# Where ff2's first blocks lie in memory, and the order in which they are loaded

## The chip, the cores and the metric

The kernel runs on one core of one Trainium2 chip. The metric is the device time of one execution in microseconds; the time before is the median of three runs. One further execution was recorded by the profiler; all rows quoted below are of that one.

The engines are TensorE (PE; its weight loads are PEld), VectorE (DVE), ScalarE (ACT), GpSimd (POOL) and SyncE (SP), whose queue issues nearly all DMAs. SBUF, the memory next to the engines, is where every tile lives; matrix products land in eight PSUM banks.

## The reference

One decoder layer on 1024 tokens of width 1024. A combined input projection feeds a recurrent group (RWKV-7, 8 heads of 64) and a causal convolution group; their outputs go through an output projection and a residual; then comes the MLP, where the change lies, and a final norm:

```python
x = x + jnp.concatenate([y_rwkv, y_conv], axis=-1) @ w_out[l]
h = rmsnorm(x, norm_mlp_g[l])
x = x + jnp.square(jax.nn.relu(h @ w_ff1[l])) @ w_ff2[l]
...
return rmsnorm(x, norm_final_g)
```

h is 1024 x 1024, w_ff1 1024 x 4096 and w_ff2 4096 x 1024, all float32. I call the two products ff1 and ff2.

## The kernel before, in words

**Precision.** A float32 product is made of three products of halves: `halves` (L848 to L853) rounds a block to a high half on ScalarE (L851) and subtracts it from the block on VectorE for the low half (L852). TensorE then multiplies high by high, high by low and low by high (L96 is the one line that issues matmuls). So every block that TensorE reads has cost one ScalarE and one VectorE instruction first: ah and al of an A block, bh and bl of a B block.

**Seven products in place of eight.** ff1 and ff2 both cut their matrices in 2 x 2 blocks and use a scheme of seven products of sums and differences (Strassen's, in Winograd's form). ff1's operand from the hidden side is kept ready split in SBUF: pool `fpa` holds the blocks B11 and B21 (mB11h, mB11l, mB21h, mB21l in the trace), pool `fpb` the sums T1 to T4 and B22. ff1 goes in 16 pairs of column blocks (`class Pair`); within a pair the products come in the order M1 (reads B11), M2 (reads B21), then M3 and M4 of the pair before, then M6, M7, M5. So in the last pair B11 and B21 are read first, and T1, B22, T4 last. Each finished block of 128 x 512 is squared ReLU on ScalarE (L871, L872) in one of three buffers `c` of pool `hd`, and written by SP to memory (L873), to one of four arrays hid_d0 to hid_d3 by the place in the 4096 hidden columns. The weights of ff1 come through four raw buffers of pool `w1p`.

**ff2.** It has four rounds r = 0 to 3, each over a quarter of the hidden columns. In round r, A is hid_d[r] and B a quarter of w_ff2; each of A11, A12, A21, A22, B11, B12, B21, B22 is loaded by `load` (L1178 to L1185 before) as two tiles c = 0, 1 of 128 x 1024 (512 KB each), with two buffers for each name. A11 and B11 have two names each, e and o, for even and odd rounds. The seven products of a round, with 48 matmuls of 128 x 512 each, are, in the program's order:

- A11·B11 and A12·B21, both added onto the output block (1,1);
- `m6`: S2·T2, where S1 = A21 + A22 and S2 = S1 - A11 are made on VectorE, T1 = B12 - B11 and T2 = B22 - T1 on GpSimd (L1189 before); added onto block (2,1);
- S1·T1, in the same banks as the product before it, then onto (2,2);
- `m7`: (A11 - A21)·(B22 - B12), then `m4`: A22·(B21 - T2), then `m3`: (A12 - S2)·B22.

`onto_x2` (L1220 before) adds a finished bank to the residual on VectorE: four instructions for each product. A product that goes on in the same bank waits for that. `ahead` issues the loads of the next round inside the round.

**Order of the work.** The program is recorded as written and then ordered by a scheduler, engine by engine, from its own cost model and from when each tile's memory is free; what stands on a queue goes out in that order. An instruction behind a waiting one on its engine waits too. SP has eight DMA semaphores in turn: a DMA waits for the one eight places before it on the queue.

**Memory.** The pools are two stacks, one from each end of SBUF. At the end of ff1 the right stack holds, from its bottom: x2 (the residual), `fpa`, `w1p`, `hd`, `fpb`. They are closed and ff2's pools are put in the same place: before, `wr` (nine names, 72 KB a partition), then `wf` (the halves ah, al, bh, bl and the sums sA, sB), then `wr3` (gf, the final norm's weights, and B11o). A new tile waits, tile by tile, until what lay in its memory has been read for the last time. Within a pool the name that was used first lies farthest from the stack's bottom: A11e, the first block that ff2 needs, lies where `hd`'s `c` buffers were, which ff1 uses to its end; A11o, needed a round later, lies on `fpa`.

Of the kernel before, what the change touches and what calls it, by code (L numbers as in the profile page):

```python
# [9 lines left out]
F32 = mybir.dt.float32  # L10
# [8 lines left out]
P = 128  # L19
# [33 lines left out]
def hymba_layer(ctx: ExitStack, tc: tile.TileContext, a: dict, out: bass.AP):  # L53
# [81 lines left out]
    right = dict(side="right", reuse_waits="tile")  # L135
# [566 lines left out]
    def open_pool(name, **kw):  # L702
        pools[name] = tc.tile_pool(name=name, bufs=1, reuse_waits="tile", **kw)
        return pools[name].__enter__()

    def close_pool(name):
        pools.pop(name).__exit__(None, None, None)
# [463 lines left out]
        close_pool(name)  # L1171


    wr = open_pool("wr", side="right")
    NR = 4
    raws = {}

    def load(r, what, i, k):  # L1178

        src = hid_d[r] if what == "A" else w_ff2_d  # L1180
        tag = f"{what}{i}{k}" + ("eo"[r % 2] if (i, k) == (1, 1) else "")
        f0, col = (4 * (k - 1), i) if what == "A" else (8 * r + 4 * (i - 1), k)
        for c in range(2):
            t = raws[r, what, i, k, c] = (wr3 if tag == "B11o" else wr).tile([P, 2, 512], F32, name=tag, bufs=2)
            nc.sync.dma_start(out=t, in_=src[:, f0 + 2 * c:f0 + 2 * c + 2, (col - 1) * 512:col * 512])  # L1185

    def sum2(engine, name, x, y, op):
# [69 lines left out]
    def quad(n):  # L1257
        return [bank(x) for x in (("ps", "ps", "ps", "pr"), ("ca", "cb", "ya", "yb"))[n % 2]]

    for args in (("A", 1, 1), ("B", 1, 1), ("A", 1, 2), ("B", 2, 1)):  # L1260
        load(0, *args)
    for args in (("A", 2, 1), ("A", 2, 2), ("B", 1, 2), ("B", 2, 2)):
        load(0, *args)
    wf = open_pool("wf", side="right")
    wr3 = open_pool("wr3", side="right")
    gf = wr3.tile([P, D], F32, name="gf")
    nc.sync.dma_start(out=gf, in_=a["norm_final_g"].partition_broadcast(P))
    for r in range(NR):
# [8 lines left out]
        def ahead(*args):  # L1277
            if not final:
                load(r + 1, *args)
# [53 lines left out]
        ahead("B", 2, 2)  # L1333
    close_pool("wr3")
    close_pool("wf")
    close_pool("wr")


_INS = ["x", "norm_mix_g", "w_in", "shift_mu", "w0", "w_decay_up", "a0", "w_aaa_up", "w_gate_up",
# [20 lines left out]
```

## Time and profile before

| | us |
|---|---|
| time before, median of three runs (1310.55 to 1310.72) | 1310.57 |
| the profiled execution's own time | 1310.69 |
| its span, first to last instruction | 1309.0 |
| TensorE busy (8107 matmuls) | 1223.2 |
| VectorE busy | 943.7 |
| ScalarE busy | 559.1 |
| GpSimd busy | 100.6 |
| ff1's last matmul starts at | 958.03 |
| ff2's first matmul starts at | 974.90 |
| ff2's last matmul starts at | 1297.76 |

All moments are counted from the span's start. A row of the timeline has the start, the duration, the engine, the line of the kernel, the operation, output <- inputs by tile name (buffer numbers left out, so ps stands for three banks), and in brackets the idle time of the engine before it with what ended that. A matmul's duration runs to the modelled end of its pipeline; its true price in a row of matmuls is the distance from start to start. "SPq" rows are DMA issues, not the transfers. In the trace all A blocks of ff2 but A11 are called A, all B blocks but B11 are called B.

### The profile page before, as it was taken

The numbers are of one execution on the slowest core, as the hardware profiler recorded it, in microseconds if no ns is written. First come the engines' busy times: TensorE is split into PE (matmuls) and PEld (weight loads), VectorE is DVE, ScalarE is ACT, GpSimd is POOL, SyncE is SP. The second block draws the span as 40 slices with busy tenths as digits, with TensorE's granted clock in tenths as the row PEclk, the third lists the DMA queues.
The fourth block names the chain that finished last, engine by engine and source line by source line (L and its number), as shares of the span: only waits on it lengthen the run. The fifth ranks groups of instructions, "written<-read, shape, count | busy, mean of one in ns | idle before, by whom it ended". The sixth has DMA issues, their size and how long they took to land.

```text
span 1309.0 us, 20808 instructions
## 1 busy us (share of the span) xinstructions
PE 1223.2 (93%) x8107; PEld 1058.3 (81%) x8107; DVE 943.7 (72%) x1639; ACT 559.1 (43%) x1001; POOL 100.6 (8%) x57
## 2 busy tenths in 40 slices
PE   5999999998998779999998999999948899999996
PEld 4999898987887668999887888888837688888885
DVE  6478796789459855655778666664429798887997
ACT  6432433433441165323577445455533233333344
POOL 1000000000000000000000000000005224232320
PEclk9999999997997587999999999999979899999998
DMA  5214426455564556533345354442266425232003
GB/s 188 57 49 108 122 66 175 106 137 128 134 168 118 124 166 182 172 105 102 93 145 185 129 163 151 152 129 98 81 226 216 145 65 161 65 96 81 17 1 129
DMA packets 194475, 161.44 MB, mean 123 GB/s; under 512 B 54386, under 2 KB 153784, under 8 KB 194376
## 3 DMA queue, kind: packets, MB, share of 16 engines
q1 hardware_dynamic: 181192, 157.90, 40.6%
q10 hardware_dynamic: 13056, 2.13, 0.9%
q8 instruction: 64, 1.05, 0.3%
q14 instruction: 35, 0.29, 0.1%
q0 software_dynamic: 128, 0.08, 0.0%
HBM read 110.23 MB, written 49.84 MB: 122 GB/s over the span
## 4 chain that ended last, share of the span: by engine, by line
PE 65%; DVE 7%; DMA 3%; ACT 2%; issue 1%; SPq 0%; ACTq 0%; DVEq 0%
PE ps L96 29%; PE yb L96 10%; PE ya L96 8%; PE cb L96 8%; PE ca L96 6%; PE pr L96 4%; DVE al L852 1%; PE ps L99 1%; DVE acc L331 1%; DVE sA L1189 1%; DMA woraw<-in_w_out_dram 1%; DVE x L1220 1%; DMA hid_d<-c 1%; DVE bl L852 1%; DVE odd L331 0%
## 5 line engine op out<-in xcount | busy, mean ns | idle before, releaser
L851 ACT ACTIVATE ah<-sA 128x1024 fp32r<-128x1024 f32 x32 | 34.0, 1061 | 135.7 <-PE pr L96 50.4
L96 PE MATMUL ps<-bh,ah 128*128 128x512 f32 x168 | 66.3, 408 | 22.4 <-ACT bh L851 16.5
L96 PE MATMUL cb<-hh,wh 128*128 128x256 f32 x248 | 72.7, 293 | 1.5 <-ACT hh L243 1.5
L96 PE MATMUL cb<-hl,wh 128*128 128x256 f32 x248 | 72.9, 294 | 0.3 <-DVE hl L244 0.3
L852 DVE TENSOR_TENSOR al<-sA,ah 128x1024 fp32r<-128x1024 f32 x32 | 55.0, 1718 | 23.5 <-ACT ah L851 23.5
L96 PE MATMUL cb<-hh,wl 128*128 128x256 f32 x248 | 71.7, 289 | 0.0
L96 PE MATMUL ps<-bl,ah 128*128 128x512 f32 x168 | 68.1, 405 | 3.7 <-DVE bl L852 3.7
L96 PE MATMUL ps<-bh,al 128*128 128x512 f32 x168 | 67.8, 403 | 0.0
L96 PE MATMUL yb<-hh,wh 128*128 128x256 f32 x232 | 67.7, 292 | 0.0
L96 PE MATMUL yb<-hh,wl 128*128 128x256 f32 x232 | 66.6, 287 | 0.0
L96 PE MATMUL yb<-hl,wh 128*128 128x256 f32 x232 | 66.5, 287 | 0.0
L851 ACT ACTIVATE w1h<-s 128x512 fp32r<-128x512 f32 x64 | 40.4, 633 | 52.6 <-PE ps L96 34.0
L852 DVE TENSOR_TENSOR w1l<-s,w1h 128x512 fp32r<-128x512 f32 x64 | 44.0, 688 | 24.8 <-ACT w1h L851 24.7
L96 PEld LDWEIGHTS ps<-bh,ah 128*128 128x128 f32 x168 | 33.0, 197 | 30.1 <-ACT bh L851 16.9
L1189 POOL TENSOR_TENSOR sB<-B,B11e 128x1024 f32<-128x1024 f32 x4 | 12.1, 3014 | 564.3 <-DMA B<-in_w_ff_dram 562.0
L871 ACT ACTIVATE c<-c 128x512 f32<-128x512 f32 x60 | 37.9, 632 | 35.6 <-DVE c L957 20.1
L96 PEld LDWEIGHTS cb<-hh,wh 128*128 128x128 f32 x248 | 48.3, 195 | 5.4 <-ACT hh L243 1.9
L96 PEld LDWEIGHTS cb<-hl,wh 128*128 128x128 f32 x248 | 48.3, 195 | 4.8 <-issue 4.0
L96 PEld LDWEIGHTS cb<-hh,wl 128*128 128x128 f32 x248 | 48.1, 194 | 2.3 <-issue 2.1
L851 ACT ACTIVATE w1h<-w1r 128x512 fp32r<-128x512 f32 x48 | 30.2, 631 | 42.5 <-PE ps L96 26.6
L852 DVE TENSOR_TENSOR w1l<-w1r,w1h 128x512 fp32r<-128x512 f32 x48 | 33.0, 689 | 19.7 <-ACT w1h L851 19.7
L96 PEld LDWEIGHTS yb<-hh,wh 128*128 128x128 f32 x232 | 44.6, 192 | 3.1 <-issue 2.1
(472 smaller groups left out, 4035.9 us busy)
## 6 DMA issues: line engine op xcount, KB each, us to landing
w1r<-in_w_ff_dram SPq DMA_DIRECT2D x44, 512.0 KB
hid_d<-c SPq DMA_DIRECT2D x64, 256.0 KB
LK<-lk_d SPq DMA_DIRECT2D x32, 384.0 KB
A<-hid_d SPq DMA_DIRECT2D x24, 512.0 KB
B<-in_w_ff_dram SPq DMA_DIRECT2D x24, 512.0 KB
wraw<-in_w_in_dram SPq DMA_DIRECT2D x22, 512.0 KB
xt<-in_x_dram SPq DMA_DIRECT2D x8, 512.0 KB
lk_d<-AR SPq DMA_DIRECT2D x16, 256.0 KB
```

The costliest lines, as they stand in the source:

```text
L96: return self._order(PE.matmul(o, lhsT=lhsT, rhs=rhs, start=start, stop=stop, skip_group_check=more))
L99: self._order(PE.transpose(o, in_, identity))
L331: return V.scalar_tensor_tensor(o, x, c, o, op0=ALU.mult, op1=ALU.add)
L851: S.activation(hi, src, AF.Copy)
L852: V.tensor_tensor(lo, src, hi.bitcast(F32), op=ALU.subtract)
L871: S.activation(c, c if src is None else src, AF.Relu)
L1189: engine.tensor_tensor(t, x, y, op=op)
L1220: V.tensor_tensor(o, o, banks[t].t, op=ALU.add)
```

## The change

Each of the nine names of `wr` gets a pool of its own, opened in the order of the list RAW, so that the first of the list lies at the bottom of the stack; and the first round's loads are issued with B12 and B22 ahead of A21 and A22 (before: behind them). Sizes and counts of tiles are the same.

```diff
-    wr = open_pool("wr", side="right")
+    RAW = ("B21", "A12", "B11e", "A11e", "A21", "B22", "B12", "A22", "A11o")
+    wr = {tag: open_pool("wr" + tag, side="right") for tag in RAW}
...
-            t = raws[r, what, i, k, c] = (wr3 if tag == "B11o" else wr).tile([P, 2, 512], F32, name=tag, bufs=2)
+            t = raws[r, what, i, k, c] = wr[tag].tile([P, 2, 512], F32, name=tag, bufs=2)
...
-    for args in (("A", 1, 1), ("B", 1, 1), ("A", 1, 2), ("B", 2, 1)):
-        load(0, *args)
-    for args in (("A", 2, 1), ("A", 2, 2), ("B", 1, 2), ("B", 2, 2)):
+    for args in (("A", 1, 1), ("B", 1, 1), ("A", 1, 2), ("B", 2, 1), ("B", 1, 2), ("B", 2, 2), ("A", 2, 1), ("A", 2, 2)):
         load(0, *args)
...
-    wr3 = open_pool("wr3", side="right")
+    wr3 = wr["B11o"] = open_pool("wr3", side="right")
...
-    close_pool("wr")
+    for tag in reversed(RAW):
+        close_pool("wr" + tag)
```

By the sizes (8 KB a partition for each name, a block of `fpa` 8 KB), B21, A12, B11e and A11e now lie on the four blocks of `fpa`, A21, B22 and B12 on `w1p`, A22 on the border of `w1p` and `hd`, and A11o on `hd`.

What the scheduler makes of it at the seam, first on SP's queue, where ff1's last writes (hid_d<-c) meet ff2's first loads. In these rows A_10043, A_10045 (now A_10067, A_10069) are A12 and B_10047, B_10049 (now B_10071, B_10073) are B21, one row for each half. Before:

```order
L873 DMA hid_d_139<-c 128x512 x10
L1267 DMA gf<-in_norm_final_g_dram 128x1024
L1185 DMA B11o<-in_w_ff_dram 128x2x512 x2
L873 DMA hid_d_139<-c 128x512
L1185 DMA A11e<-hid_d_136 128x2x512 x2
L1185 DMA B11e<-in_w_ff_dram 128x2x512 x2
L1185 DMA A_10043<-hid_d_136 128x2x512
L1185 DMA A_10045<-hid_d_136 128x2x512
L1185 DMA B_10047<-in_w_ff_dram 128x2x512
L1185 DMA B_10049<-in_w_ff_dram 128x2x512
```

And now:

```order
L873 DMA hid_d_139<-c 128x512 x5
L1186 DMA A11e<-hid_d_136 128x2x512 x2
L1186 DMA B11e<-in_w_ff_dram 128x2x512 x2
L1186 DMA A_10067<-hid_d_136 128x2x512
L873 DMA hid_d_139<-c 128x512
L1186 DMA A_10069<-hid_d_136 128x2x512
L1186 DMA B_10071<-in_w_ff_dram 128x2x512
L1186 DMA B_10073<-in_w_ff_dram 128x2x512
L873 DMA hid_d_139<-c 128x512 x4
```

The four blocks of the first two products stand ahead of the last six writes of ff1 (one of those comes further down); the rows of gf and B11o are behind them.

On ScalarE, at the same place, the splits of A11 and B11 (ah, bh) beside ff1's last activations (c). Before:

```order
L871 ACTIVATE c<-ps 128x512
L872 ACTIVATE c<-c 128x512
L871 ACTIVATE c<-c 128x512
L872 ACTIVATE c<-c 128x512
L851 ACTIVATE ah<-A11e 128x1024 x2
L851 ACTIVATE bh<-B11e 128x1024 x2
```

And now:

```order
L871 ACTIVATE c<-ps 128x512
L872 ACTIVATE c<-c 128x512
L851 ACTIVATE ah<-A11e 128x1024
L851 ACTIVATE bh<-B11e 128x1024
L851 ACTIVATE ah<-A11e 128x1024
L851 ACTIVATE bh<-B11e 128x1024
L851 ACTIVATE ah<-A_10067 128x1024
L851 ACTIVATE bh<-B_10071 128x1024
L871 ACTIVATE c<-c 128x512
L872 ACTIVATE c<-c 128x512
```

Six splits moved ahead of ff1's last block, and the halves of A11 and B11 now take turns.

The second place is the sums of round 0. On SP's queue A_10053 is the second half of A21, A_10055 and A_10057 are A22, B_10059 and B_10061 B12, B_10063 and B_10065 B22. Before:

```order
L1185 DMA A_10053<-hid_d_136 128x2x512
L1185 DMA A_10055<-hid_d_136 128x2x512
L1185 DMA A_10057<-hid_d_136 128x2x512
L1185 DMA B_10059<-in_w_ff_dram 128x2x512
L1185 DMA B_10061<-in_w_ff_dram 128x2x512
L1185 DMA B_10063<-in_w_ff_dram 128x2x512
L1185 DMA B_10065<-in_w_ff_dram 128x2x512
L1185 DMA A11o<-hid_d_137 128x2x512 x2
L1185 DMA B11e<-in_w_ff_dram 128x2x512
```

And now, where A_10085 is the second half of A21 and A_10087, A_10089 are A22 (B12 and B22 went out before these rows):

```order
L1186 DMA A_10085<-hid_d_136 128x2x512
L1266 DMA gf<-in_norm_final_g_dram 128x1024
L1186 DMA B11o<-in_w_ff_dram 128x2x512 x2
L1186 DMA B11e<-in_w_ff_dram 128x2x512
L873 DMA hid_d_139<-c 128x512
L1186 DMA B11e<-in_w_ff_dram 128x2x512
L1186 DMA A_10087<-hid_d_136 128x2x512
L1186 DMA A_10089<-hid_d_136 128x2x512
L1186 DMA A11o<-hid_d_137 128x2x512 x2
```

Ahead of A22 stand now gf, B11o, the B11 of round 2 (B11e; it goes into the buffer that round 0's B11 still holds, and waits for the last reader of each half, VectorE and GpSimd) and ff1's last write.

On VectorE, from the last splits of the second product to S2 of the first half (x_0 to x_3 are the residual's updates, sA<-A,A is S1, sA<-sA,A11e is S2, bl<-sB the low half of T2). Before:

```order
L852 TENSOR_TENSOR al<-A_10045,ah 128x1024
L1220 TENSOR_TENSOR x_0_4867<-x_0_4867,ps 128x512
L852 TENSOR_TENSOR bl<-B_10049,bh 128x1024
L1189 TENSOR_TENSOR sA<-A_10051,A_10055 128x1024
L1220 TENSOR_TENSOR x_1_4868<-x_1_4868,ps 128x512
L1220 TENSOR_TENSOR x_2_4869<-x_2_4869,ps 128x512
L1189 TENSOR_TENSOR sA<-sA,A11e 128x1024
```

And now:

```order
L852 TENSOR_TENSOR al<-A_10069,ah 128x1024
L852 TENSOR_TENSOR bl<-B_10073,bh 128x1024
L1221 TENSOR_TENSOR x_0_4867<-x_0_4867,ps 128x512
L1221 TENSOR_TENSOR x_1_4868<-x_1_4868,ps 128x512
L1221 TENSOR_TENSOR x_2_4869<-x_2_4869,ps 128x512
L1221 TENSOR_TENSOR x_3_4870<-x_3_4870,pr 128x512
L852 TENSOR_TENSOR bl<-sB,bh 128x1024
L1190 TENSOR_TENSOR sA<-A_10083,A_10087 128x1024
L1190 TENSOR_TENSOR sA<-sA,A11e 128x1024
```

The four updates and the low half of T2 now stand ahead of S1 and S2; before, two of the updates and that low half came behind.

## Prediction

> **What bounds the kernel now.** I read the page first (busy shares), then the stretches of 10 us, then the TensorE timeline at every gap, and from each gap the engine that ended it. The page's first two lines say that TensorE carries the program; the stretches around the seam between ff1 and ff2 say where it does not (columns: PE, PEld, DVE, ACT, POOL busy us, granted clock, DMA share, GB/s).
>
> ```profile
> span 1309.0 us, 20808 instructions
> ...
> PE 1223.2 (93%) x8107; PEld 1058.3 (81%) x8107; DVE 943.7 (72%) x1639; ACT 559.1 (43%) x1001; POOL 100.6 (8%) x57
> ...
> 950.00:960.00 10.00, 7.74 (x33) 5.74 (x31) 1.83 (x3) 3.87 (x7) 0.00 (x0) 1.00 0.14 52
> 960.00:970.00 10.00, 0.00 (x0) 0.00 (x0) 0.00 (x0) 1.15 (x2) 0.00 (x0) 0.66 0.74 245
> 970.00:980.00 10.00, 5.10 (x12) 4.04 (x13) 6.13 (x5) 5.41 (x6) 0.00 (x0) 0.50 1.03 374
> ...
> 1000.00:1010.00 10.00, 6.53 (x22) 4.93 (x21) 10.00 (x9) 3.90 (x4) 2.78 (x2) 0.83 0.47 157
> 1010.00:1020.00 10.00, 5.99 (x26) 4.30 (x24) 10.00 (x6) 3.85 (x4) 6.58 (x2) 1.00 0.51 152
> 1020.00:1030.00 10.00, 7.86 (x23) 6.27 (x24) 8.99 (x10) 0.27 (x1) 3.89 (x2) 0.66 0.71 235
> 1030.00:1040.00 10.00, 10.00 (x46) 8.29 (x45) 5.52 (x7) 4.02 (x4) 0.88 (x1) 1.00 0.09 34
> ```
>
> There are two holes. From 958 to 975 nothing computes and DMA works: ff2's first blocks are loading. From 1000 to 1030 VectorE is full (10.00 of 10) and TensorE is not: the sums of ff2's round 0. After 1030 TensorE has no gap of note (46 matmuls in 10 us). The TensorE timeline has the gaps; the row in brackets names who ended it.
>
> ```profile
> 958.03 0.39 PE L96 MATMUL ya<-mT4h,w1l 128*128 128x512 f32 x1
> 974.90 1.65 PE L96 MATMUL ps<-bh,ah 128*128 128x512 f32 x3 [16.48 <-ACT bh L851]
> ...
> 976.77 0.63 PE L96 MATMUL ps<-bl,ah 128*128 128x512 f32 x1
> 977.20 0.63 PE L96 MATMUL ps<-bh,al 128*128 128x512 f32 x1
> ...
> 982.96 0.39 PE L96 MATMUL ps<-bh,ah 128*128 128x512 f32 x1
> 983.18 0.39 PE L96 MATMUL ps<-bl,ah 128*128 128x512 f32 x1
> ...
> 999.28 0.84 PE L96 MATMUL ps<-bh,ah 128*128 128x512 f32 x3
> ...
> 1003.81 0.54 PE L96 MATMUL ps<-bl,ah 128*128 128x512 f32 x1 [3.47 <-DVE bl L852]
> ...
> 1022.14 0.76 PE L96 MATMUL ps<-bh,ah 128*128 128x512 f32 x1 [5.90 <-DVE x L1220]
> ```
>
> One matmul takes 0.227 us from start to start at full clock (982.96 to 983.18, rounded) and 0.43 at half (976.77 to 977.20). I call the products by their order: P1 = A11·B11 and P2 = A12·B21 (974.90 to 999.28), P3 = S2·T2 from 999.28, P4 = S1·T1 from 1022.14; each has 48 matmuls, 10.9 us at full clock.
>
> Why the first gap is 16.5 us stands on SP's queue and in the chain of waits.
>
> ```profile
> 959.17 0.33 SPq L1267 DMA_DIRECT2D gf<-in_norm_final_g_dram  x1
> ...
> 960.59 7.46 DMA hid_d<-c
> ...
> 968.52 5.25 DMA B11e<-in_w_ff_dram
> ...
> 973.79 1.07 ACT bh L851
> ```
>
> gf, then two blocks of the next round, then ff1's last output go out before A11; the second half of A11 waits for that output to be written (960.59 + 7.46), B11 goes out behind it at 968.52 and lands 5.25 us later. All of it begins after ff1's last matmul.
>
> **The change, part by part.**
>
> *Loads move into ff1.* A11, B11, A12, B21 now lie where ff1's B11 and B21 blocks were, whose last reader is the TensorE row here, beside a row of SP's queue, one of VectorE and the DMA's:
>
> ```profile
> 938.02 0.39 PE L96 MATMUL cb<-mB21h,w1l 128*128 128x512 f32 x1
> ...
> 937.40 5.66 SPq L873 DMA_DIRECT2D hid_d<-c  x3
> ...
> 952.66 0.69 DVE L957 TENSOR_TENSOR c<-u,ya 128x512 f32<-128x512 f32 x1 [2.21 <-ACT u L927]
> ...
> DMA  0000000000100000580000291008500005800000
> ```
>
> SP reaches them behind the write at 937.40, so eight 512 KB loads go out between about 938 and 942, into an almost idle DMA (the last row is its busy share from 930 to 950, in tenths). In the stretch 970 to 980 DMA moved 374 GB/s, 1.4 us a load: landed by about 951. Six microseconds are in hand before ScalarE wants them (957, below). What it could cost: the ff1 writes queued among them land later, by at most eight times 1.4 = 11 us. The next output is written at 952.66, into a buffer whose write was queued near 941: 11 us of cover. I cost it at nothing; without the cover ff1 would lose the few us by which the write is late, and no gain is possible, since ff1 ends on TensorE.
>
> *The start of ff2.* ScalarE now has six splits ahead of ff1's last activation, behind the one before it.
>
> ```profile
> 955.74 0.60 ACT L871 ACTIVATE c<-ps 128x512 f32<-128x512 f32 x1 [1.06 <-PE ps L96]
> 956.37 0.63 ACT L872 ACTIVATE c<-c 128x512 f32<-128x512 f32 x1
> ...
> 982.93 1.06 ACT L851 ACTIVATE ah<-A 128x1024 fp32r<-128x1024 f32 x1 [2.67 <-PE pr L96]
> 983.90 1.04 ACT L851 ACTIVATE bh<-B 128x1024 fp32r<-128x1024 f32 x1
> ```
>
> 957.00 + 0.97 + 1.04 = 959.01: P1 starts at 959.05 instead of 974.90, **-15.85 us**. The output that now waits behind the six splits is needed in round 3 alone.
>
> *P1 and P2* are paced by VectorE's low halves. These rows give its prices and POOL's:
>
> ```profile
> 958.46 0.69 DVE L973 TENSOR_TENSOR c<-u,ya 128x512 f32<-128x512 f32 x1 [5.11 <-PE ya L96]
> ...
> 995.32 2.82 DVE L852 TENSOR_TENSOR al<-sA,ah 128x1024 fp32r<-128x1024 f32 x1
> 998.07 3.42 DVE L1189 TENSOR_TENSOR sA<-sA,A11e 128x1024 f32<-128x1024 f32 x1
> ...
> 1010.15 1.21 DVE L852 TENSOR_TENSOR bl<-sB,bh 128x1024 fp32r<-128x1024 f32 x1
> 1011.28 1.21 DVE L852 TENSOR_TENSOR al<-sA,ah 128x1024 fp32r<-128x1024 f32 x1
> ...
> 1021.32 1.27 DVE L1220 TENSOR_TENSOR x<-x,ps 128x512 f32<-128x512 f32 x2
> ...
> 987.48 2.91 POOL L1189 TENSOR_TENSOR sB<-B,B11e 128x1024 f32<-128x1024 f32 x1 [561.95 <-DMA B<-in_w_ff_dram]
> ...
> 997.13 3.27 POOL L1189 TENSOR_TENSOR sB<-B,sB 128x1024 f32<-128x1024 f32 x1
> ...
> 1003.84 2.38 POOL L1312 TENSOR_TENSOR sB<-B,sB 128x1024 f32<-128x1024 f32 x1 [3.44 <-DVE bl L852]
> ```
>
> A split or sum of 128x1024 costs VectorE 1.14 us from start to start, an update of x 0.6, a POOL sum 2.4 when alone. Where they meet they take turns: the sum that began at 998.07 beside POOL's of 997.13 ended 1.1 us after POOL's end at 1000.40. So I add the two engines' times wherever POOL has work.
>
> Two low halves stand behind ff1's last sum (958.46 + 0.6): 959.1 + 2 x 1.14, ended at 961.5. The four matmuls that need only high halves are out by 959.95, so P1 waits 1.5 us there. The start of P2 waits about 1.8 more, since POOL's sums now fall among the splits (in before POOL began at 987.48, behind all eight). P1 and P2 end at 984, 25.0 us after 959.05; before they took 24.4, of which 2.6 went to the half clock.
>
> *P3.* POOL needs B12, which SP sends at 957.6, behind ff1's last write but one, and which lands by 961.5. VectorE must do, from 959.1: eight low halves, four updates, one low half of sB and S1, S2 of the first chunk, 11 x 1.14 + 4 x 0.6 = 14.9; POOL in between T1, T2 of both chunks and the first sum of m4, 5 x 2.4 = 12.0. S2 is there at 986.0, its high half 1.06 later: P3 starts at 987.2, not at 999.28. That is -12.1: **3.8 us of the gain are given back here.** A22, which S1 needs, goes out late: SP stands at the second B11 of round 2 until POOL's third sum (two turns of VectorE and three of POOL behind 962.5: about 972), sends A22 at 972.5, and it lands by 977 to 980, for a need at 981.4. That cover is 1 to 4 us; every us beyond it moves P3 one for one.
>
> *P4* waits for the update of x that empties its bank. Between S2 and that update VectorE has eleven more splits and sums and four updates, 14.9, and POOL one and a half turns, 3.6: 986.0 + 18.5 + 0.7 = 1005.3, instead of 1022.14: **-16.8 us.** So P3, which took 22.9 us with its stalls, takes 18.1; this is the second term of the sum, -4.7 from 987.2.
>
> *The clock.* After the 5.90 us gap P4 ran at half clock to 1028 (0.66 granted in 1020 to 1030: 6.8 of those 10 us at half): 5.9 us, in which 14 matmuls cost 0.2 too much, 2.8 us. After: no wait near P4 is over 3.4 us, but P3 is only 60% busy. The row of 1010 to 1020 has 5.99 busy at clock 1.00, that of 1000 to 1010 6.53 at 0.83, so neither end is sure: between 0 and 2.8 I take -1.5. [...]
>
> *Rounds 1 to 3* keep their work and their engines have room (TensorE 10.00 of 10 from 1030): 0, or up to 1 us either way where a load is queued differently.
>
> Sum: -15.85 + 3.8 - 4.7 - 1.5 = -18.3. Against the profiled execution (1310.69, span 1309.0, 0.12 over the median of 1310.57): **1292.4 us.**
>
> **Rivals.**
>
> 1. *POOL and VectorE do not hold each other up.* Then VectorE is never late: P3 follows P2 at 959.05 + 1.5 + 21.8 = 982.4, P4 at 993.3, and 28.8 + 2.8 us are gained: 1279. For it: the split at 1011.28 beside no POOL row costs 1.21. Against it: 2.82 and 3.42 above. [...] Chance 0.06.
>
> 2. *The sums take back more.* POOL wins more turns, or A22 lands after 981.4, and P3 and P4 come 4 to 7 us later than I count: 1296 to 1300. For it: rows of 2.82 and 3.42 are the rule while POOL runs, and A22 now stands behind a wait on POOL. Against: the number of sums is the same. Chance 0.12.
>
> 3. *The loads do not come early.* If SP does not reach A11 before ff1's end, the gap stays: 1310.6, no change. Against: the row order of SP and the last reader at 938.02. Chance 0.03.
>
> 4. *Slower.* SP's wait for POOL's sum with A22 behind it. TensorE needs S1 = A21 + A22 in P3; A22's lateness passes to the end one for one once it lands after 981.4, and the change loses when it lands more than 18 us after that, at 1000, which asks that POOL's third sum end at 995 rather than 972. POOL's rows above are 2.4 to 3.3 us each; it would have to be shut out by VectorE's whole queue. Five us past that point are 1316. Chance 0.02.
>
> **How the numbers follow.** Forecast 0.77, rivals 0.06, 0.12, 0.03, 0.02. Range: the clock term (0 to 2.8) and 1 us for rounds 1 to 3 make 1290 to 1295; A22's cover and the turns at the port add 3 us on both sides, and rival 2 reaches in to 1299: 1287 to 1299. About 0.2%, 2.6 us, is what can be told from no change. Faster by more than that 0.95, same 0.03, slower 0.02.
>
> **What would show it.** Right: A11e loads issued near 938, P1's first matmul near 959, P3's near 987 ended by ScalarE's ah or VectorE, P4's near 1005 ended by an update of x. Wrong: a gap over 3 us behind 958, P3 before 984 (rival 1), SP's A22 issue after 976 or P4 after 1009 (rival 2), a slower ff1 before 958.

## The result, and the profile after

The changed kernel takes 1291.38 us (median of 4 runs, 1289.46 to 1293.33) where the kernel before took 1310.64 beside it (4 runs, 1310.55 to 1311.39): a ratio of 0.9845, 95% interval 0.9823 to 0.9867. The profiled execution took 1291.95 us, its span is 1290.2.

The stretches around the seam, with the same columns as before (PE, PEld, DVE, ACT, POOL busy us, granted clock, DMA share, GB/s):

```profile
950.00:960.00 10.00, 8.80 (x38) 6.67 (x37) 2.40 (x4) 5.81 (x9) 0.00 (x0) 1.00 0.59 201
960.00:970.00 10.00, 8.66 (x38) 6.83 (x37) 10.00 (x6) 6.38 (x8) 6.84 (x3) 1.00 1.01 366
...
980.00:990.00 10.00, 6.51 (x23) 4.54 (x21) 9.97 (x8) 2.00 (x2) 6.53 (x2) 0.85 0.44 156
990.00:1000.00 10.00, 6.79 (x29) 5.20 (x29) 10.00 (x8) 4.02 (x4) 3.33 (x2) 0.98 0.44 121
...
1010.00:1020.00 10.00, 10.00 (x46) 8.28 (x45) 7.66 (x9) 4.02 (x4) 3.32 (x1) 1.00 0.54 196
```

The first hole, the empty stretch from 958 to 975, is gone: TensorE works through it at full clock (granted 1.00 from 950 to 980), but for waits of 0.53 and 1.34 us. The second is still there, some 18 us earlier (P4 starts at 1004.33 and not at 1022.14): from 980 to 1000 VectorE is full and TensorE has 6.5 to 6.8 of 10. From 1010 on TensorE is full. TensorE's gaps, all of 0.2 us and more up to 1040:

```profile
959.47 0.96 PE L96 MATMUL ps<-bh,ah 128*128 128x512 f32 x3 [0.53 <-ACT bh L851]
...
962.00 0.50 PE L96 MATMUL ps<-bl,ah 128*128 128x512 f32 x1 [1.34 <-DVE bl L852]
...
986.68 0.50 PE L96 MATMUL ps<-bh,ah 128*128 128x512 f32 x1 [3.49 <-ACT ah L851]
...
991.18 0.50 PE L96 MATMUL ps<-bh,al 128*128 128x512 f32 x1 [1.01 <-DVE al L852]
...
999.10 0.50 PE L96 MATMUL ps<-bh,al 128*128 128x512 f32 x1 [2.20 <-DVE al L852]
...
1004.33 0.47 PE L96 MATMUL ps<-bh,ah 128*128 128x512 f32 x1 [1.30 <-DVE x L1221]
...
1007.56 0.50 PE L96 MATMUL ps<-bh,ah 128*128 128x512 f32 x1 [0.27 <-DVE x L1221]
...
1027.19 0.47 PE L96 MATMUL ca<-bh,ah 128*128 128x512 f32 x1 [0.26 <-DVE x L1221]
```

P1 starts at 959.47, P3 at 986.68, P4 at 1004.33. Why P3 and P4 wait is seen where VectorE's rows (first) and GpSimd's (last three) are laid beside each other:

```profile
959.59 1.22 DVE L852 TENSOR_TENSOR al<-A11e,ah 128x1024 fp32r<-128x1024 f32 x1
...
964.13 3.42 DVE L852 TENSOR_TENSOR al<-A,ah 128x1024 fp32r<-128x1024 f32 x1
...
974.16 3.41 DVE L852 TENSOR_TENSOR bl<-B,bh 128x1024 fp32r<-128x1024 f32 x1
...
981.02 1.21 DVE L1190 TENSOR_TENSOR sA<-A,A 128x1024 f32<-128x1024 f32 x1
982.26 3.27 DVE L1190 TENSOR_TENSOR sA<-sA,A11e 128x1024 f32<-128x1024 f32 x1
...
1003.51 0.67 DVE L1221 TENSOR_TENSOR x<-x,ps 128x512 f32<-128x512 f32 x1
...
963.08 3.39 POOL L1190 TENSOR_TENSOR sB<-B,B11e 128x1024 f32<-128x1024 f32 x1 [539.29 <-DVE al L852]
...
973.23 3.26 POOL L1190 TENSOR_TENSOR sB<-B,sB 128x1024 f32<-128x1024 f32 x1
...
981.18 3.28 POOL L1311 TENSOR_TENSOR sB<-B,sB 128x1024 f32<-128x1024 f32 x1 [4.69 <-DVE bl L852]
```

A low half alone takes 1.22; the four of P2 (964.13 to 974.16), beside GpSimd's T1 and T2 (963.08 to 973.23), take 3.41 or 3.42 each, and S2 (982.26) takes 3.27 beside GpSimd's next sum. P3 waits for S2. P4 waits for the update of x at 1003.51, which stands 18.05 us behind S2 on VectorE's queue (985.46 to 1003.51): eleven splits and sums and four updates, 14.9 us, and 3.1 us in which two of these splits wait for GpSimd. SP's queue shows the rest:

```profile
938.34 0.94 SPq L1186 DMA_DIRECT2D A11e<-hid_d  x2
...
957.96 1.96 SPq L1186 DMA_DIRECT2D B<-in_w_ff_dram  x4
...
973.59 0.98 SPq L1186 DMA_DIRECT2D A<-hid_d  x2
```

A11 goes out at 938.34, B12 and B22 at 957.96, A22 at 973.59, and S1 at 981.02 did not wait for it.

**One scale for all kernels.** The moment at which ff1 ends differs between executions of the same instructions by several us (shown at the end). So I count from ff1's last sum on VectorE (line 973: 958.46 before, 958.98 after) to the first matmul of P1, P3 and P4 and to the last matmul of the program, always in the profiled execution; what comes after that sum is where the kernels differ.

| us behind ff1's last sum | P1 | P3 | P4 | last matmul |
|---|---|---|---|---|
| before | 16.44 | 40.82 | 63.68 | 339.30 |
| after; again | 0.49; 0.48 | 27.70; 27.72 | 45.35; 45.38 | 320.03; 319.69 |
| pools alone; again | 0.49; 0.49 | 25.95; 26.85 | 43.63; 44.53 | 317.37; 318.72 |
| order of loads alone | 16.53 | 41.98 | 59.39 | 332.51 |
| after, no GpSimd sums in round 0 | 0.49 | 25.38 | 39.27 | 314.96 |
| before, no GpSimd sums in round 0 | 16.50 | 40.52 | no gap | 326.83 |
| after, round 0's sums on VectorE | 0.48 | 25.27 | 41.42 | 315.81 |
| after, all sums on VectorE | 0.48 | 25.87 | 42.03 | 315.12 |
| pools alone, all sums on VectorE | 0.49 | 25.89 | 42.05 | 316.54 |
| after, T1 and T2 made twice | 0.49 | 32.04 | 55.20 | 328.75 |
| after, eight updates of x left out | 0.49 | 25.70 | 43.30 | 316.03 |
| pools alone, A22 behind one wait | 0.49 | 25.89 | 43.56 | 317.75 |

The change takes 19.27 us off this distance (339.30 - 320.03), and 19.26 off the median.

### The profile page after: what moved, and what is told of

It is laid out like the page before. It is cut to its first block, busy times and chain, and to the rows that moved or that the text cites. A ratio compares the mean times of both kernels' runs of the same rounds, so it can differ in the third digit from the quotient of the medians.

```text
span 1290.2 us, 20800 instructions
## 1 busy us (share of the span) xinstructions
PE 1217.5 (94%) x8107; PEld 1052.2 (82%) x8107; DVE 944.8 (73%) x1639; ACT 558.0 (43%) x1001; POOL 107.4 (8%) x57
## 4 chain that ended last, share of the span: by engine, by line
PE 61%; DVE 9%; DMA 4%; ACT 2%; issue 1%; SPq 0%; ACTq 0%; DVEq 0%
PE ps L96 27%; PE yb L96 9%; PE ya L96 8%; PE cb L96 7%; PE ca L96 6%; PE pr L96 3%; DVE bl L852 2%; DVE al L852 2%; DVE sA L1190 1%; DVE x L1221 1%; PE ps L99 1%; DMA woraw<-in_w_out_dram 1%; DMA th_d<-QS 1%; DVE Q L530 1%; DVE Qt L528 1%
## 5 line engine op out<-in xcount | busy, mean ns | idle before, releaser
L96 PE MATMUL ps<-bh,al 128*128 128x512 f32 x168 | 65.0, 391 | 3.2 <-DVE al L852 3.2
L852 DVE TENSOR_TENSOR al<-sA,ah 128x1024 fp32r<-128x1024 f32 x32 | 48.0, 1506 | 19.6 <-ACT ah L851 19.5
L1190 POOL TENSOR_TENSOR sB<-B,B11e 128x1024 f32<-128x1024 f32 x4 | 12.5, 3134 | 541.6 <-DVE al L852 539.3
L96 PEld LDWEIGHTS yb<-hh,wl 128*128 128x128 f32 x232 | 44.6, 192 | 1.6 <-issue 1.5
```

The source lines that it names most:

```text
L96: return self._order(PE.matmul(o, lhsT=lhsT, rhs=rhs, start=start, stop=stop, skip_group_check=more))
L852: V.tensor_tensor(lo, src, hi.bitcast(F32), op=ALU.subtract)
L1190: engine.tensor_tensor(t, x, y, op=op)
```

## The experiments

Theory: the early loads remove the first hole; in what is left VectorE's queue sets P3 and P4, and each GpSimd sum costs it a turn. Rivals: the order of the loads carries part of the gain; A22's late load sets P3; the two engines don't hold each other up.

### Each half of the change alone

Pools apart, the loads in their old order:

```diff
-    for args in (("A", 1, 1), ("B", 1, 1), ("A", 1, 2), ("B", 2, 1), ("B", 1, 2), ("B", 2, 2), ("A", 2, 1), ("A", 2, 2)):
+    for args in (("A", 1, 1), ("B", 1, 1), ("A", 1, 2), ("B", 2, 1)):
+        load(0, *args)
+    for args in (("A", 2, 1), ("A", 2, 2), ("B", 1, 2), ("B", 2, 2)):
```

> The nine pools with the loads of round 0 in their old order (A21 and A22 ahead of B12 and B22). Theory (the pools bring the whole gain, and from 959 on VectorE's and GpSimd's sums taking turns set the pace, whatever the order in which the last four blocks land): first product at 959, the fourth at 1002 to 1007, 1289 to 1293 us, within 2 us of the changed kernel. Rival (the order of the loads carries the later part): GpSimd starts four loads later, 4 x 1.4 = 5.6 us, the third and fourth product come 5 us later, 1296 to 1298 us.

Measured: 1290.12 us, ratio 0.983 (0.9812 to 0.9848). It ran once more as a mark for a later kernel:

> The kernel with the pools apart and the loads in their old order once more, as the mark for the run with A22 earlier. Both theories: 1289 to 1291.5 us; third product 25.95 and fourth 43.6 behind ff1's last sum.

Measured: 1290.65 us, ratio 0.9842 (0.9823 to 0.9861). The pools alone bring the whole gain; by the distance they are 1.0 to 2.7 us better than the whole change, though the intervals of the times overlap. VectorE's, GpSimd's and SP's rows of the first of these:

```profile
981.90 1.23 DVE L1190 TENSOR_TENSOR sA<-A,A 128x1024 f32<-128x1024 f32 x1 [4.61 <-DMA A<-hid_d]
...
966.89 2.45 POOL L1190 TENSOR_TENSOR sB<-B,B11e 128x1024 f32<-128x1024 f32 x1 [541.83 <-DMA B<-in_w_ff_dram]
...
976.48 0.98 SPq L1186 DMA_DIRECT2D A<-hid_d  x2
```

GpSimd starts 6.82 us behind P1's first matmul (960.07 here) and not 3.61, so only the last two of the eight first low halves meet its sums. But here VectorE waits 4.61 us for A22: the wait that the prediction counted as covered is the one that ends last ahead of S1 in this kernel. What stands behind it is shown by the last of the kernels below.

The old single pool, B12 and B22 loaded ahead of A21 and A22 (against the kernel before):

```diff
-    for args in (("A", 1, 1), ("B", 1, 1), ("A", 1, 2), ("B", 2, 1)):
-        load(0, *args)
-    for args in (("A", 2, 1), ("A", 2, 2), ("B", 1, 2), ("B", 2, 2)):
+    for args in (("A", 1, 1), ("B", 1, 1), ("A", 1, 2), ("B", 2, 1), ("B", 1, 2), ("B", 2, 2), ("A", 2, 1), ("A", 2, 2)):
```

> The old single pool with B12 and B22 loaded ahead of A21 and A22. Theory: nothing leaves the gap behind ff1, the first product stays at 974.9; GpSimd starts some us earlier and takes its turns earlier, the fourth product at 1019 to 1023: 1307 to 1311 us. Rival (the order carries the part of the gain that is made after the first product, 18.8 - 15.9 = 2.9 us, and more since B12 is there 5.6 us sooner): 1302 to 1306 us.

Measured: 1306.88 us, ratio 0.9957 (0.9941 to 0.9973). It lies just under the theory's range and above the rival's; by the distance, 6.79 us, the rival is nearer: in the old pool the order has a gain of its own. On the scale of the profile before P4 comes at 1017.85, ahead of the theory's 1019 to 1023. TensorE and GpSimd:

```profile
1020.79 0.47 PE L96 MATMUL ps<-bh,ah 128*128 128x512 f32 x1 [0.62 <-DVE x L1220]
...
985.38 2.41 POOL L1189 TENSOR_TENSOR sB<-B,B11e 128x1024 f32<-128x1024 f32 x1 [558.21 <-PE pr L96]
```

GpSimd starts 7.45 us behind P1 (977.93 here) where it was 12.58 before (987.48 - 974.90), its turns are over sooner, and the gap of 5.90 ahead of P4 is 0.62: P4 comes 4.29 us earlier, and without the half clock that followed the long gap (matmuls last 0.39 there; the remaining 2.5). So the two halves do not add up: 20.6 to 21.9 and 6.8 alone, 19.3 to 19.6 together. With the pools apart the new order only makes GpSimd start earlier than it should.

### GpSimd's turns

Round 0 without GpSimd's sums, in the kernel after and in the kernel before (B12, B22 and B21 are used in their place, in the fifth and sixth product too):

```diff
-            T1[c] = sum2(G, "sB", B(1, 2, c), B(1, 1, c), ALU.subtract)
+            T1[c] = B(1, 2, c) if r == 0 else sum2(G, "sB", B(1, 2, c), B(1, 1, c), ALU.subtract)
...
-            T2[c] = sum2(G, "sB", B(2, 2, c), T1[c], ALU.subtract)
+            T2[c] = B(2, 2, c) if r == 0 else sum2(G, "sB", B(2, 2, c), T1[c], ALU.subtract)
```

> The changed kernel with round 0's sums on GpSimd left out: B12, B22 and B21 are used in the place of T1, T2 and the sums made of them, so the output is not the reference's. Theory (GpSimd's sums hold VectorE up, 12.0 us of turns before the third product): VectorE has 14.9 us of work from 959.1 and is never late for it; the third product follows the second at 981 to 984 instead of 987, the fourth comes at 993 to 999 instead of 1004.3: 1280 to 1286 us. Rival (VectorE's own work, or A22 landing late, sets the pace): the fourth product stays at 1002 to 1005, 1289 to 1292 us.

Measured: 1287.48 us, ratio 0.9807 (0.9785 to 0.9828). By the distance 5.1 us are gained, a little less than the least expected: P4 at 39.27 (998.3 on the scale of the profile after) is at the late edge of its range, and P3 at 25.38 (984.4) behind its. VectorE's row and SP's say why:

```profile
982.75 1.23 DVE L1190 TENSOR_TENSOR sA<-A,A 128x1024 f32<-128x1024 f32 x1 [4.51 <-DMA A<-hid_d]
...
971.57 1.86 SPq L1186 DMA_DIRECT2D A<-hid_d  x2
```

With the turns gone, S1 waits 4.51 us for A22, which went out at 971.57 and had landed at 982.75, 20.15 behind ff1's last sum (962.60 here). That is a second floor, 2 us under the first (S1 stood at 22.04 in the profile after). The turns are what P3 waits for, but only 2 us deep.

> The kernel before with the same sums of round 0 left out (output not the reference's). Theory: the first product stays at 974.9; the stalls of 3.47 and 5.90 us in front of and in the third and fourth product shrink and the half clock behind them (2.8 us) with them: 1297 to 1303 us. Rival (in the kernel before, the blocks that land late set the pace of round 0, not the sums): 1308 to 1311 us.

Measured: 1299.57 us, ratio 0.9905 (0.9882 to 0.9928). As expected, with 12.5 us by the distance. As in the kernel before, P1 begins at half clock behind the first hole (here to 986.4), but P2, P3 and P4 have neither a gap nor half clock; the next gap is one of 1.71 us at 1040.15, ahead of the sixth product. The stretches (and one from an earlier stage, for the end of this document):

```profile
300.00:340.00 40.00, 35.37 (x334) 30.37 (x334) 34.81 (x58) 15.54 (x36) 0.11 (x1) 0.74 0.56 130
...
1000.00:1010.00 10.00, 10.00 (x46) 8.29 (x45) 10.00 (x12) 4.02 (x4) 0.00 (x0) 1.00 0.47 154
1010.00:1020.00 10.00, 10.00 (x46) 8.29 (x45) 10.00 (x12) 4.03 (x4) 0.00 (x0) 1.00 0.69 208
```

The opposite test, T1 and T2 of round 0 made twice:

```diff
+            if r == 0:
+                G.tensor_tensor(T1[c], B(1, 2, c), B(1, 1, c), op=ALU.subtract)
...
+            if r == 0:
+                G.tensor_tensor(T2[c], B(2, 2, c), T1[c], op=ALU.subtract)
```

> The changed kernel with T1 and T2 of round 0 made twice on GpSimd, the second time over the first, so four sums more on GpSimd and nothing else. Theory (every GpSimd sum that meets VectorE's work takes a turn of about 2.3 us from it): 4 x 2.3 = 9.2 us; the third product starts 36 to 38 behind ff1's last sum instead of 27.7, the fourth at 53 to 57 instead of 45.4: 1299 to 1303 us. Rival (GpSimd's sums run beside VectorE and cost it nothing; the four sums only use up the 4.69 and 2.29 us for which GpSimd waits now): the third product at 28 to 31, 1291 to 1295 us.

Measured: 1301.41 us, ratio 0.9927 (0.991 to 0.9944). VectorE's rows and TensorE's:

```profile
962.80 3.41 DVE L852 TENSOR_TENSOR bl<-B11e,bh 128x1024 fp32r<-128x1024 f32 x1
...
989.61 3.38 DVE L1190 TENSOR_TENSOR sA<-A,A 128x1024 f32<-128x1024 f32 x1
...
990.83 0.80 PE L96 MATMUL ps<-bh,ah 128*128 128x512 f32 x1 [5.71 <-ACT ah L851]
...
1012.12 0.80 PE L96 MATMUL ca<-bh,ah 128*128 128x512 f32 x1 [7.05 <-ACT bh L851]
...
1013.99 0.63 PE L96 MATMUL ps<-bh,ah 128*128 128x512 f32 x1
```

Up to S2's end seven of VectorE's instructions are held up, the first at 962.80, where five were, and the next at 989.61: of the four sums more, two fall ahead of S2. P3 is 4.3 us later, the price of two turns of 2.2, and not the 8 to 10 expected; P4 is 9.85 later, about that of four (8.8), and the last matmul 8.7. TensorE's order changed too (the fifth product, into ca, begins 1.9 us ahead of P4), so P4's moment is not quite the same thing here. The time is the theory's, and the rival's 1291 to 1295 is out.

### The same sums on VectorE

Nothing is left out here: only the engine changes, beside a second run of the changed kernel.

```diff
-            T1[c] = sum2(G, "sB", B(1, 2, c), B(1, 1, c), ALU.subtract)
+            T1[c] = sum2(V if r == 0 else G, "sB", B(1, 2, c), B(1, 1, c), ALU.subtract)
```

and so for T2, the fifth product's sum and the sixth's; in the second and third kernel `V` in every round, in the third with the loads in their old order as well.

> The changed kernel once more, as the mark for the three others. Both theories: 1289 to 1293 us; third product 27.7 us and fourth 45.4 us behind ff1's last sum on VectorE, last matmul 320.0 behind it.

Measured: 1291.83 us, ratio 0.9841 (0.9829 to 0.9854).

> The changed kernel with GpSimd's eight sums of round 0 (T1, T2, and those of the fifth and sixth product) made on VectorE instead; nothing is left out. Theory (a sum on GpSimd costs VectorE a turn of 2.4 us, and 1.14 us if VectorE makes it itself): six to seven turns, 15.6 us, ahead of the fourth product become 8 us; it can't come before the third is done, about 39 behind ff1's last sum as it did with the sums left out: 39.5 to 43 instead of 45.4, and 1285 to 1289 us. Rival (GpSimd takes work off VectorE, whose own queue sets the pace): eight more sums of 1.14 us on VectorE put the fourth product at 48 or later: 1293 to 1297 us.

Measured: 1288.27 us, ratio 0.9811 (0.9797 to 0.9824): 3.6 us under the changed kernel beside it, and the intervals do not overlap. P4 is at 41.42, inside the theory's range. By the distance this kernel is also 1.6 to 2.9 us shorter than the one with the pools alone, though the intervals of those times overlap. TensorE's rows and VectorE's:

```profile
985.23 0.50 PE L96 MATMUL ps<-bh,ah 128*128 128x512 f32 x1 [1.07 <-ACT ah L851]
...
989.34 0.50 PE L96 MATMUL ps<-bh,al 128*128 128x512 f32 x1 [2.00 <-DVE al L852]
...
990.84 0.39 PE L96 MATMUL ps<-bl,ah 128*128 128x512 f32 x1
...
979.99 1.23 DVE L1190 TENSOR_TENSOR sA<-A,A 128x1024 f32<-128x1024 f32 x1 [0.39 <-DMA A<-hid_d]
```

P3's wait is down to 1.07 (3.49 after), and S1 is again at the floor of A22: 0.39 us of wait, 20.03 behind ff1's last sum (959.96).

> The changed kernel with these sums on VectorE in all four rounds; GpSimd makes none in ff2. Theory (rounds 1 to 3 have no gap on TensorE that VectorE or GpSimd could close: from the fourth product on, 274.7 us for 25 products of 10.9 = 272.5): at most 2.2 us below the run with round 0 alone: 1284 to 1288 us. Rival (VectorE, with 28 splits, 28 updates and 16 sums a round, 28 x 1.14 + 28 x 0.6 + 16 x 1.14 = 67 of 76 us, is too full where the sums stand close together): a stall of 2 to 3 us in each round, 1290 to 1296 us.

Measured: 1288.22 us, ratio 0.9814 (0.9797 to 0.983), a little over the theory's range and far under the rival's; 0.7 us less than with round 0 alone by the distance. Rounds 1 to 3 neither gain nor lose that can be told.

> Pools apart, the loads of round 0 in their old order (A21 and A22 first), and these sums on VectorE in all rounds. Theory (the old order was better with the pools apart because GpSimd then began its turns later, among fewer splits; without GpSimd's turns the order is worth nothing): within 1.5 us of the run with the new order and all sums on VectorE. Rival (the order is worth 2.7 us by itself, through A21 and A22 for S1): 2 to 3 us faster than that.

Measured: 1287.55 us, ratio 0.9819 (0.9794 to 0.9844); by the distance 1.4 us more than with the new order. Without GpSimd's turns the order of the loads has no gain left in it that can be told, as the theory said.

### VectorE's own queue, and A22

The residual's updates by P1 and P2 of round 0 left out:

```diff
-        product(alpha, True, lambda c: (A(1, 1, c), B(1, 1, c)), then=lambda t: onto_x2(1, 1, alpha, t))
+        product(alpha, True, lambda c: (A(1, 1, c), B(1, 1, c)), then=lambda t: r and onto_x2(1, 1, alpha, t))
```

and the same in the line of P2.

> The changed kernel with the updates of the residual by the first two products of round 0 left out (the output is not the reference's): eight VectorE instructions of 0.6 us less, four of them ahead of S2. Theory (VectorE's whole queue, its own work and the turns, is what the third and fourth product wait for): the third product 2.4 us earlier, at 25.3, the fourth 3 to 5 us earlier, at 40.5 to 42.5: 1286 to 1289 us. Rival (the third product waits for T2 from GpSimd, or for A22, not for VectorE's queue): third product at 27 to 28, 1290 to 1292 us.

Measured: 1290.42 us, ratio 0.9837 (0.9816 to 0.9858), over the expected time; by the distance 4.0 us are gained. P3 is at 25.70, as the theory has it; P4 at 43.30 is not. TensorE's rows and VectorE's:

```profile
983.23 0.50 PE L96 MATMUL ps<-bh,ah 128*128 128x512 f32 x1 [0.57 <-ACT ah L851]
...
1000.83 0.47 PE L96 MATMUL ps<-bh,ah 128*128 128x512 f32 x1 [2.10 <-DVE x L1221]
...
977.59 3.23 DVE L1190 TENSOR_TENSOR sA<-A,A 128x1024 f32<-128x1024 f32 x1 [0.34 <-DMA A<-hid_d]
...
984.26 3.39 DVE L852 TENSOR_TENSOR al<-sA,ah 128x1024 fp32r<-128x1024 f32 x1
...
997.74 1.21 DVE L1190 TENSOR_TENSOR sA<-A11e,A 128x1024 f32<-128x1024 f32 x1
...
1000.01 0.68 DVE L1221 TENSOR_TENSOR x<-x,ps 128x512 f32<-128x512 f32 x1
```

With the whole 4.8 us gained P4 would have come 2.75 us sooner. Three things make up nearly all of that: S1 waits 0.34 for A22 (977.59); the scheduler filled the room with work of the fifth product, the sum of 997.74, which now stands ahead of the update that P4 waits for (1.14); and a turn of GpSimd falls on the whole of the low half of 984.26 (3.39), where in the changed kernel the same low half took 2.20 (1.2). VectorE's queue sets P4, with its order and the turns in it.

Last, A22 in the kernel with the pools alone. The second half of round 2's B11 gets a buffer of its own, so that SP has one wait less ahead of A22:

```diff
+            own = (r, what, i, k, c) == (2, "B", 1, 1, 1)
-            t = raws[r, what, i, k, c] = wr[tag].tile([P, 2, 512], F32, name=tag, bufs=2)
+            t = raws[r, what, i, k, c] = (wr3.tile([P, 2, 512], F32, name="B11g") if own else
+                                          wr[tag].tile([P, 2, 512], F32, name=tag, bufs=2))
```

> Pools apart with the loads in their old order, and the second half of the B11 block of round 2 in a buffer of its own, so that A22 stands behind one wait for GpSimd on SP's queue (to about 969.8 us) instead of two (976.5). In the kernel with the pools alone VectorE waited 4.61 us for A22. Theory (that wait was on the path): A22 goes out at 970 and has landed by 976, S1 follows the low half of sB without a wait, the third product starts at 24.2 to 25 behind ff1's last sum instead of 25.95, the fourth at 39 to 41.5 instead of 43.6: 1286 to 1289 us. Rival (VectorE's idle 4.61 us would only be spent waiting for GpSimd's sums a little later): the fourth product at 43 to 44, 1289.5 to 1291.5 us.

Measured: 1290.59 us, ratio 0.9841 (0.9823 to 0.9859): no gain over the pools alone beside it (1290.65). The time and P4 at 43.56 are the rival's. The theory failed at its first step, the landing of A22. SP, VectorE, GpSimd, and the stretches:

```profile
967.85 1.35 SPq L1188 DMA_DIRECT2D A<-hid_d  x2
...
978.43 2.61 DVE L1192 TENSOR_TENSOR sA<-A,A 128x1024 f32<-128x1024 f32 x1 [3.09 <-DMA A<-hid_d]
...
977.55 2.40 POOL L1315 TENSOR_TENSOR sB<-B,sB 128x1024 f32<-128x1024 f32 x1
```

```profile
960.00:970.00 10.00, 9.44 (x41) 7.80 (x42) 8.73 (x7) 4.95 (x6) 4.74 (x2) 1.00 1.03 388
970.00:980.00 10.00, 10.00 (x46) 8.27 (x45) 6.91 (x7) 2.13 (x2) 9.88 (x4) 1.00 1.05 390
```

A22 was sent 10.30 us behind ff1's last sum and not 16.90, and landed at 20.88 and not at 22.32: 6.6 us earlier out, 1.4 earlier in (2.3 against the second run of the pools alone, 23.22). And what was won there went to GpSimd, as the rival had it: S1 takes 2.61 beside the sum of 977.55, where with the pools alone it took 1.23, so that it ends 23.49 behind ff1's last sum and not 23.55. The DMA is full from 960 to 980 (390 GB/s, 1.34 us for each 512 KB). In the six kernels in which A22 went out 9 to 13.5 us behind ff1's last sum and S1 waited for it, it landed at 20.0 to 20.9 whatever the moment of its issue. What stands ahead of it there is B12, B22, A21, but also gf, B11o and round 2's B11, which nobody needs yet. To send A22 ahead of these was not tried.

## Why the prediction was right, point by point

- **P1 starts 15.85 us earlier:** 15.95. The six splits ran where the prediction had them; ff1's last sum came 0.52 later, less than it moves between executions.
- **P1 and P2 in 25.0 us:** 23.7 (986.68 - 3.49 - 959.47). P1 waited 1.34 (predicted 1.5). The 1.8 us at the start of P2 were mis-sized: 0.62 in one profile of the changed kernel, no row in the other; GpSimd began at 963.08, behind the first low half of P1's second chunk. On the path it cost nothing either way: P2 was through 3.49 us ahead of P3, which waits for VectorE's S2.
- **P3, 3.8 us given back:** 2.8 (15.95 - 13.12). VectorE's 14.9 were right: the time from 959.59 to S2's end at 985.53 is 25.9, of which the five GpSimd turns are 11.0. A turn costs 2.2 us and not 2.4: the 3.42 of a held-up low half less the 1.22 of a free one. The rows fit two engines that each wait for one instruction of the other: the low half of 964.13 ends at 967.55, 1.08 us behind the end of GpSimd's sum of 963.08 (966.47), and that sum takes 3.39 where the one of 1003.84 in the kernel before took 2.38. Through what they hold each other up is not shown: no run shows the port that the prediction's range speaks of, only the turns, here the five of 2.2 us. Making the sums twice showed a turn by its price.
- **P3 in 18.1 us, so P4 16.8 earlier:** 17.65, and P4 18.33 earlier, 1 us of it the point before. VectorE's 14.9 from S2 to the update were right again; the turns were 3.1 and not 3.6.
- **The clock, -1.5:** P4 ran at full clock (granted 1.00 from 1000 to 1020), and the whole 2.8 came back. But from P4 to the last matmul only 0.94 is gained (275.62 to 274.68). The other 1.9 went to short waits that the kernel before does not have: counted from the distances of the matmuls' starts beyond 0.227, 0.55 us at 1006.90, 0.51 at 1026.54, 0.44 at 1125.19 and 0.38 at 1201.87. The first two are P4 and the sixth product waiting for VectorE's updates; the last two lie in rounds 2 and 3, which the sum put at nothing.
- **A22's cover, 1 to 4 us:** sent at 973.59 (predicted 972.5), not waited for. Since S1 did not wait, no row shows when it landed. Sent 9 to 13.5 us behind ff1's last sum it had landed at 20.0 to 20.9, sent at 16.9 (the pools alone) at 22.3 and 23.2; here it was sent at 14.6, and S1's turn is at 22.04. By these a cover of 2 us at most, an estimate. What the prediction had wrong is why it is late: behind SP's wait stands a full DMA (a share of 1.01 from 960 to 970, of 1.00 from 970 to 980).
- **Rivals.** That the engines don't hold each other up is ruled out by the doubled sums. (The row that was counted for it, the low half of 1011.28 in the profile before, is not free of GpSimd: a sum of 3.32 us starts at 1011.44, and there it is the one that waits.) The sums took back less, not more. The loads came early. The slower case did not come near, but its place is real: with the pools alone VectorE stood 4.61 and 5.52 us for A22.
- **The order of the loads** had no term of its own in the sum, and should have had one: alone it is worth 6.8 us, on top of the pools it costs 1.0 to 2.7.
- **The sum:** -18.3 against 19.27 us gained by the distance. The terms missed by 0.1 (P1), 1.0 (P3), 0.5 (P4) and, the other way, 0.6 (the clock). The last offsets a part of the others, so a little of the time's closeness is luck; no term was right by another's error.

## What to carry to other kernels

When a transfer is moved ahead of a hole, ask what becomes due next and list all floors there: here TensorE's own work (24 us), a block's landing behind a full DMA (20 us, then 5 us of sums and splits), and VectorE's queue with GpSimd's turns lay within 4 us of each other, so taking one away paid only down to the next. A helper engine that takes turns with VectorE is no help where VectorE is on the path: here a sum on GpSimd took 2.2 us from VectorE, which makes it itself in 1.14. Two edits that each gain alone can take from each other; run each alone.

## What the runs showed of the hardware

**The clock after short waits.** In the kernel before, half clock followed the gaps of 16.48, 3.47 and 5.90 us. In the other kernels it followed some gaps of 2.0 to 2.7 us, and not others of that length. With all sums on VectorE:

```profile
991.08 0.50 PE L96 MATMUL ps<-bh,al 128*128 128x512 f32 x1 [2.01 <-DVE al L852]
...
992.36 0.63 PE L96 MATMUL ps<-bh,ah 128*128 128x512 f32 x1
992.79 0.63 PE L96 MATMUL ps<-bl,ah 128*128 128x512 f32 x1
```

From 1.3 us behind this gap of 2.01 on, matmuls last 0.63 and follow each other at 0.43, until 995.76; in the kernel with round 0's sums on VectorE a gap of 2.00 at the same place (989.34) is followed by full clock (0.39 at 990.84). A gap of 2.38 (pools alone, 990.02) and one of 2.68 (round 0 on VectorE, 1001.38) cost the half clock, one of 2.20 (after, 999.10) did not. In the kernel with the doubled sums even the wait of 1.33 us within P1 did (half clock from 962.44 to 965.78); the same wait in the other kernels did not. So no length of gap parts the two kinds: half clock once followed 1.33, and did not follow 2.20. The two stretches at half clock with moments here last 3.40 us (992.36 to 995.76) and 3.34 (962.44 to 965.78), about 1.6 us lost in each, an estimate from the distance of 0.43 against 0.227. What decides which of two nearly equal gaps costs the half clock was not shown.

**The moment at which ff1 ends.** The same instructions up to there (6763 matmuls, 1316 of VectorE's) took up to 6.7 us longer in some executions (965.11 in the kernel before without GpSimd's sums, 958.46 in the kernel before). The kernel before, in a stretch of an earlier stage:

```profile
300.00:340.00 40.00, 36.32 (x365) 31.00 (x365) 35.57 (x60) 16.64 (x40) 0.11 (x1) 0.83 0.55 127
```

There 365 matmuls at a granted clock of 0.83, in the other execution 334 at 0.74 in the same 40 us (its row stands above). From 500 to 600 it is 891 matmuls at 0.97 against 870 at 0.94. Since single times carry this with them (1289.46 to 1293.33 for the changed kernel), differences of 1 to 3 us were read from the distance behind ff1's last sum.
